# Elementwise work moved between engines, one-hot rows built by fours, a re-priced instruction planner, and 1200 unread products on TensorE

## The chip, the cores and the metric

The kernel runs on one core of one Trainium2 chip. The metric is the device time of one execution in microseconds (us), from launch to the last result, as the median of several executions. Engines are named as in the profile: PE is TensorE (PEld its weight loads), DVE is VectorE, ACT is ScalarE, POOL is GpSimd, SP is SyncE, whose queue issues most DMA transfers.

## What is computed

Two layers of a small transformer over 256 latent tokens and 256 context tokens, width 1024. In layer 0 both streams pass a token mixer and a PEER feed-forward layer; in layer 1 the context passes only as much of the mixer as the latents read.

```python
def peer_ffn(h, wq, keys, u_tab, v_tab):
    ...
    q = (t @ wq).reshape(n, PEER_HEADS, 2, PEER_HALF)
    s = jnp.einsum('thcd,cnd->thcn', q, keys).astype(F32)
    sv, si = lax.top_k(s, PEER_TOPK)
    cand = (sv[:, :, 0, :, None] + sv[:, :, 1, None, :]).reshape(n, PEER_HEADS, PEER_TOPK * PEER_TOPK)
    cv, ci = lax.top_k(cand, PEER_TOPK)
    ...
        act = jax.nn.gelu(jnp.einsum('pd,ped->pe', tb, u_tab[eb]), approximate=False)
        return jnp.einsum('pe,ped->pd', act * gb, v_tab[eb])

def reference(...):
    for l in range(DEPTH):
        ...
        m, mc = token_mixer(h, hc, ...)          # three branches and a gated merge
        x = x + gt1 * m
        x = x + gt2 * peer_ffn(modulate(x, norm2_g[l], sh2, sc2), ...)
        if need_ctx:
            xc = xc + gt1c * mc
            xc = xc + gt2c * peer_ffn(modulate(xc, norm2_g[l], sh2c, sc2c), ...)
    return x
```

The mixer's branches are a differential attention (A), a windowed attention with a sink (B) and a gated delta rule over chunks (C). PEER picks 128 of 16,384 experts for each token; an expert is one row of `u_tab` and one of `v_tab`, 4 KB each.

## The kernel before

**Work and stages.** A matrix product in full precision is three products of halves: `split` (627) copies an operand on ACT into a rounded half `hi`, and a `tensor_tensor` subtraction gives the rest `lo`, on DVE or, where the caller says so, on POOL; `mm3` (651) then multiplies hi by hi, hi by lo and lo by hi. Weights come in tiles of 128x1024 (512 KB) from the SP queue. The stages follow each other as: mixer of the context in layer 0; its PEER routing (label "01 route" in this text: the context route); mixer of the latents in layer 0 while the context's experts are gathered; the latents' route and dense PEER in layer 0 beside the rest of the gathers; the context part of layer 1; the latents' mixer, route and dense PEER of layer 1.

**Gathered PEER (context, `peer_gather` 1638).** For each of two token blocks, 128 indirect DMAs on POOL fetch rows of `u_tab` into tiles `rows`, each followed by one product with a running sum on DVE (`scalar_tensor_tensor` rows<-rows,ga); then 128 indirect DMAs fetch rows of `v_tab`, which PE multiplies with small masks into `ps`. These phases are called U0, V0, U1, V1.

**Dense PEER (latents, `peer_dense` 1531).** All experts are computed: for each pair of expert tiles `first` (1545) loads two tiles of `u_tab`, splits them and makes 48 products of 256 columns (dU); later two tiles of `v_tab` are loaded and split, and 24 products of 512 columns are summed into four PSUM banks (dV). `pre` pairs of dU are done ahead of the first dV. What an expert weighs for a token is a matrix that `weights` (1500) builds: for each token one row of two one-hot vectors on DVE (`tensor_scalar` against `iota`, 128 columns) and one 128x128 product on PE, copied out on ACT and written to memory. This is the build.

**The order of the work.** Nothing is issued directly. `Rec` (280) records every operation, and `order` (386) plans all five engines' queues at once with priced operations (`cost`), priorities, a limited number of buffers (tags b4, b2, b1 in SBUF, ps in PSUM) and lanes; each engine then runs its queue in order, held by semaphores. `BORROW` lends buffers of one tag to the gather. NEAR, FAR, SPARE limit how far an operation may run ahead of its lane. An instruction's line in the profile is thus always that of the emitting helper, 603; groups are told apart by names and shapes.

**What the change touches.** The subtraction of a split on POOL: mixer weights by `wpool` (WPOOL, 47 of them, from the layer-0 latents' misc stage to their route), dU tiles by `up` (UP1, 32 in layer 1), dV tiles by VP (112 in layer 1). `gdn_chains` (1020), seven chains of the delta rule, scales 128x256 tiles by per-head columns on POOL (144 of them). `aux`, set to POOL for layer 1, does the small sums of `route` and the products in `decode`. `qk_prep`, `out_proj` add on POOL.

## Time and profile before

| | us |
|---|---|
| median of 3 executions | 3939.72 (3938.74 to 3962.46) |
| the profiled execution | 3933.92 |
| its span, first to last instruction | 3932.1 |
| PE busy | 3530.0 (90%) |
| DVE busy | 2472.8 (63%) |
| ACT busy | 1610.0 (41%) |
| POOL busy | 1481.9 (38%) |
| mean granted PE clock | 0.933 |

The profiled execution is read as the time of the kernel: span plus 1.8 us around it. A busy engine is one that has an instruction in flight; a product that streams at half clock counts as busy for twice as long. Idle time of PE is shown with the engine whose result ended it. Where stretches are named by A:B, they are us from the span's start.

### The profile page before, as it was taken

What the parts mean: (1) busy time and instruction counts of PE and PEld (TensorE: products, weight loads), DVE (VectorE), ACT (ScalarE), POOL (GpSimd) and SP (SyncE); (2) the same over time, 40 slices, a digit from 0 to 9 for tenths busy, and PEclk for the clock granted to TensorE, in tenths of its full rate; (3) what the DMA queues carried; (4) which work ended last, traced back from release to release, by engine and by line L of the source; (5) the groups of instructions that cost most, each with busy time, mean ns of one, the idle gap of its engine ahead of it and who ended that gap; (6) DMA issues with size and microseconds to landing.
All of it is one profiled execution on the core that took longest, in us unless ns stands there. A gap on an engine that the chain in (4) does not pass through costs nothing. (4 is left out here: it accounts for less than half of the span.)

```text
span 3932.1 us, 64402 instructions
## 1 busy us (share of the span) xinstructions
PE 3530.0 (90%) x24312; PEld 2982.5 (76%) x24312; DVE 2472.8 (63%) x5599; ACT 1610.0 (41%) x3070; POOL 1481.9 (38%) x1125
## 2 busy tenths in 40 slices
PE   7999964986997798889999999998996899899999
PEld 6787954866794467767777888877896699678998
DVE  4444579889656886897444454646559942555554
ACT  4544422433442233343333346544543343344443
POOL 1110123778364345663333202222023043675443
PEclk9999986877898999999999998988998999999999
DMA  7356742566466799999889851302351455565653
GB/s 279 112 169 239 254 168 98 184 230 233 161 206 231 252 368 376 384 409 361 334 332 333 310 195 43 103 28 89 103 197 65 129 184 170 190 222 213 221 207 142
DMA packets 300966, 837.78 MB, mean 213 GB/s; under 512 B 26736, under 2 KB 96752, under 8 KB 300656
## 3 DMA queue, kind: packets, MB, share of 16 engines
q1 hardware_dynamic: 153168, 522.80, 37.2%
q0 software_dynamic: 73728, 268.47, 18.6%
q10 hardware_dynamic: 73760, 42.40, 3.6%
q8 instruction: 192, 3.15, 0.3%
q14 instruction: 118, 0.97, 0.1%
HBM read 792.67 MB, written 40.89 MB: 212 GB/s over the span
## 5 line engine op out<-in xcount | busy, mean ns | idle before, releaser
L603 PE MATMUL ps<-b,b 128*128 128x256 f32 (+4 forms) x18528 | 2742.4, 309 | 202.7 <-DVE b L603 134.8
L603 PEld LDWEIGHTS ps<-b,b 128*128 128x128 f32 (+2 forms) x18528 | 2449.7, 192 | 476.8 <-DVE b L603 163.3
L603 DVE TENSOR_TENSOR b<-b,b 128x1024 fp32r<-128x1024 f32 (+3 forms) x1065 | 1142.8, 1106 | 817.2 <-ACT b L603 550.9
L603 ACT CAST b<-b 128x1024 fp32r<-128x1024 f32 (+1 forms) x982 | 917.4, 976 | 702.6 <-PE ps L603 297.9
L603 POOL TENSOR_TENSOR b<-b,b 128x1024 fp32r<-128x1024 f32 (+2 forms) x241 | 586.8, 2445 | 922.7 <-DVE b L603 367.5
L603 ACT COPY b<-ps 128x256 f32<-128x256 f32 (+3 forms) x896 | 291.2, 350 | 676.4 <-PE ps L603 666.6
L603 POOL DMA_INDIRECT rows<-in_u_tab,eid x256 | 357.8, 1398 | 271.1 <-DVE rows L603 118.2
L603 POOL DMA_INDIRECT rows<-in_v_tab,eidT x256 | 284.0, 1109 | 426.5 <-PE ps L603 354.6
L603 PE MATMUL ps<-b 128*128 128x128 f32 (+1 forms) x2048 | 337.9, 320 | 19.2 <-ACT b L603 7.5
L603 PE MATMUL ps<-consts,b 128*128 128x128 f32 (+1 forms) x1290 | 261.1, 316 | 103.8 <-DVE b L603 76.9
L603 ACT ACTIVATE b<-ps 128x512 f32<-128x512 f32 (+1 forms) x264 | 136.7, 520 | 523.5 <-PE ps L603 507.0
L603 PEld LDWEIGHTS ps<-b 128*128 128x128 f32 (+1 forms) x2048 | 255.7, 207 | 119.6 <-DVE b L603 39.6
L603 DVE SCALAR_TENSOR_TENSOR rows<-rows,ga 128x1024 f32<-128x1024 f32 x256 | 322.9, 1288 | 4.4 <-DMA rows<-in_u_tab,eid 2.4
L603 PEld LDWEIGHTS ps<-consts,b 128*128 128x128 f32 x1290 | 184.4, 180 | 148.2 <-issue 68.8
L603 DVE TENSOR_SCALAR b<-consts,b 128x128 f32<-128x128 f32 x1024 | 235.4, 309 | 10.8 <-DMA gd<-b 7.7
L603 PE MATMUL ps<-rows,ga 128*32 128x512 f32 x1024 | 160.5, 626 | 19.0 <-DMA rows<-in_v_tab,eidT 17.8
L603 DVE COPY_PREDICATED b<-masks,ps 128x64 f32<-128x64 uint8 (+1 forms) x416 | 83.7, 251 | 148.5 <-PE ps L603 146.9
L603 ACT COPY b<-b 128x128 f32<-128x128 f32 x384 | 108.0, 303 | 60.5 <-DVE b L603 56.1
L603 DVE TENSOR_TENSOR b<-ps,b 128x128 f32<-128x128 f32 (+4 forms) x144 | 61.9, 454 | 93.8 <-PE ps L603 57.8
L603 PEld LDWEIGHTS ps<-rows,ga 128*32 128x32 f32 x1024 | 29.5, 111 | 94.6 <-DMA rows<-in_v_tab,eidT 47.8
L603 PE MATMUL ps<-b,cs 128*32 128x256 f32 x768 | 69.8, 430 | 12.2 <-DVE cs L603 11.5
L603 ACT ACTIVATE b<-b 128x512 f32<-128x512 f32 (+1 forms) x62 | 38.9, 629 | 96.0 <-DVE b L603 42.5
(176 smaller groups left out, 1450.6 us busy)
## 6 DMA issues: line engine op xcount, KB each, us to landing
b<-in_u_cols SPq DMA_DIRECT2D x256, 512.0 KB
b<-in_v_tab SPq DMA_DIRECT2D x256, 512.0 KB
b<-in_w_in SPq DMA_DIRECT2D x184, 512.0 KB
gd<-b ACTq DMA_DIRECT2D x64, 512.0 KB
b<-gd SPq DMA_DIRECT2D x64, 512.0 KB
b<-in_w_ada SPq DMA_DIRECT2D x48, 512.0 KB
b<-in_w_ada SPq DMA_DIRECT2D x96, 256.0 KB
b<-in_wq SPq DMA_DIRECT2D x48, 512.0 KB
```

The source lines that it names most:

```text
L603: r = getattr(getattr(nc, o.eng), o.meth)(*[_real(x) for x in o.args], **{k: _real(x) for k, x in o.kw.items()})
```

## The change

Splits are all on DVE (WPOOL, UP0, UP1 empty, VP 1), as are the additions of `qk_prep` and `out_proj` and the small sums of layer 1's route. The chains' scalings become two ACT instructions of 128 columns in place of one POOL instruction of 256. One-hots are built four tokens at a time: the first vector of four tokens in one DVE `tensor_tensor`, three of the four second vectors by DVE as before, the fourth by two ACT instructions (Abs, Relu). The planner prices operations anew, knows of a port between DVE and POOL, gives borrowed slots back earlier, lets marked operations run ahead of FAR, and has other limits; PRE is 32 in place of 48. One PSUM bank is taken from `ps` (8 to 7) for products of two constant tiles that nothing reads; `rests` counts them from the planner's own idle time of PE, and `emit` puts them ahead of the product that is to wait.

```diff
-WPOOL = (1, 3, 5, 7)
-UP0, UP1 = (), range(0, 64, 4)
+WPOOL = ()
+UP0, UP1 = (), ()
-OUTV = False
+OUTV = True
-VP = 8
+VP = 1
+
+ACTB = (1, 1)
+TAIL, FREE1 = 0, True
+FREE = {"b4": 4, "b2": 2, "b1": 1, "ps": 0}
-PRE = 48
+PRE = 32
+WARM0, WARM = 20.0, 0.75
-NEAR, FAR = 20.0, 150.0
+NEAR, FAR, URGENT = 20.0, 80.0, 0.0
...
+        o.port = eng in ("vector", "gpsimd") and not o.dma and sum(
+            isinstance(x, V) and x.n > 1 and x.tile.kind == "sb" for x in ins) > 1
...
+    def rests(self, order):
+
+        out, end = {}, 0.0
+        for when, i in order:
+            o = self.ops[i]
+            if o.eng == "tensor":
+                if when > WARM0:
+                    out[i] = int(max(0.0, when - end - 0.3) * WARM / 0.24)
+                end = when + o.dur
+        return out
+
     def emit(self):
...
+            for _ in range(rests.get(i, 0)):
+                nc.tensor.matmul(bank, w.real(), x.real(), start=True, stop=True)
...
-        self.bufs = {"ps": 8, "psg": 2, "b4": B4, "b2": B2, "b1": B1}
+        self.bufs = {"ps": 7, "psg": 2, "b4": B4, "b2": B2, "b1": B1}
...
-                nc.gpsimd.tensor_tensor(m1, M1[:, None, :].to_broadcast([P, H2, P]), bc(gc), op=OP.mult)
+                for h in range(H2):
+                    nc.scalar.activation(m1[:, h], M1, AF.Copy, scale=gc[:, h:h + 1])
...
+                nc.vector.tensor_tensor(A[:, :, 0], io4, sc[:, 1, k:k + 4, None].to_broadcast([P, 4, P]), op=OP.is_equal)
                 for t in range(4):
                     k = t0 + q + t
-                    nc.vector.tensor_scalar(A[:, t, 0], self.iota, sc[:, 1, k:k + 1], None, OP.is_equal)
-                    nc.vector.tensor_scalar(A[:, t, 1], self.iota, sc[:, 0, k:k + 1], sc[:, 2, k:k + 1],
-                                            OP.is_equal, OP.mult)
+                    if t >= ACTB[l]:
+                        nc.vector.tensor_scalar(A[:, t, 1], self.iota, sc[:, 0, k:k + 1], sc[:, 2, k:k + 1],
+                                                OP.is_equal, OP.mult)
+                    else:
+
+                        d = A[:, t, 1]
+                        nc.scalar.activation(d, self.iota, AF.Abs, scale=-1.0, bias=sc[:, 0, k:k + 1])
+                        nc.scalar.activation(d, d, AF.Relu, scale=sc[:, 3, k:k + 1], bias=sc[:, 2, k:k + 1])
...
-        self.aux = self.nc.gpsimd
+        pass
         self.lab("1 norm1")
+        self.nc.free = FREE1
```

Counted in the built program: POOL has 1130 instructions before and 721 after, DVE 4913 and 4666, ACT 3046 and 3592, PE 21074 and 23474 (1200 products into `warm` and as many weight loads). Of the 1200, 217 stand in two runs in the context route (155 and 62), 162 in layer 1's route (160 of them in one run), 159 in 18 places before V0's products, 160 in 29 places in layer 0's dense PEER, and the other 502 in places of at most 34.

**The build in layer 1, DVE's queue.** `b` tiles are the one-hots, `consts` the iota. Before:

```order
L603 TENSOR_TENSOR b_5773_30349<-io_8_159,pjf_30347 128x1024
L603 TENSOR_SCALAR b_5787_30357<-consts_71,b_5777_30336 128x128 x4
L603 TENSOR_SCALAR b_5789_30362<-consts_71,b_5777_30336 128x128 x4
L603 TENSOR_SCALAR b_5791_30367<-consts_71,b_5777_30336 128x128 x2
L603 TENSOR_REDUCE pii_29622<-b_5774_30355 128x2x16 x2
```

After, DVE and then ACT:

```order
L642 TENSOR_TENSOR pgw_31668<-pgw_31668,psm_31685 128x256
L642 TENSOR_TENSOR b_5791_31648<-consts_72,b_5781_31646 128x4x128
L642 TENSOR_TENSOR b_5793_31652<-consts_72,b_5781_31646 128x4x128
L642 TENSOR_SCALAR b_5791_31648<-consts_72,b_5781_31646 128x128 x3
L642 TENSOR_SCALAR b_5793_31652<-consts_72,b_5781_31646 128x128 x3
```

```order
L642 ACTIVATE b_5845_31976<-consts_72,b_5781_31646 128x128
L642 ACTIVATE b_5845_31976<-b_5845_31976,b_5781_31646 128x128
L642 COPY b_5829_31955<-ps_31970 128x64x4
L642 COPY b_5830_31960<-ps_31970 128x64x4
L642 ACTIVATE b_5847_31990<-consts_72,b_5781_31646 128x128
L642 ACTIVATE b_5847_31990<-b_5847_31990,b_5781_31646 128x128
```

Eight DVE instructions for four tokens became four, and ACT got two beside its two copies out of PSUM.

**The dV stretch of layer 1, DVE's queue.** A 128x1024 row is the subtraction of a tile's split, the 128x2x128 and 128x512 rows are the weights' product and split for a pair. Before (the other tiles' subtractions are in POOL's queue):

```order
L603 TENSOR_TENSOR b_6534_35213<-b_6534_35213,b_6536_35030 128x2x128
L603 TENSOR_TENSOR b_6538_35246<-b_6534_35213,b_6537_35235 128x512
L603 TENSOR_TENSOR b_6552_35276<-b_6552_35276,b_6535_35012 128x2x128
L603 TENSOR_TENSOR b_6552_35276<-b_6552_35276,b_6536_35030 128x2x128
L603 TENSOR_TENSOR b_6554_35296<-b_6552_35276,b_6553_35289 128x512
L603 TENSOR_TENSOR b_6567_35302<-b_6565_35207,b_6566_35293 128x1024
```

After:

```order
L642 TENSOR_TENSOR b_6604_36754<-b_6604_36754,b_6606_36356 128x2x128
L642 TENSOR_TENSOR b_6634_36777<-b_6632_36526,b_6633_36744 128x1024
L642 TENSOR_TENSOR b_6608_36791<-b_6604_36754,b_6607_36773 128x512
L642 TENSOR_TENSOR b_6622_36811<-b_6622_36811,b_6605_36316 128x2x128
L642 TENSOR_TENSOR b_6622_36811<-b_6622_36811,b_6606_36356 128x2x128
L642 TENSOR_TENSOR b_6624_36829<-b_6622_36811,b_6623_36824 128x512
L642 TENSOR_TENSOR b_6637_36851<-b_6635_36566,b_6636_36795 128x1024
```

All subtractions stand in one queue now, and POOL's has none.

**The context route, PE's queue.** PE has done the hi parts of a projection and needs the `lo` of a weight tile (b_1358), which DVE makes. Before:

```order
L603 MATMUL ps_6422<-b_1201_4431,b_1331_6412 128x128 x4
L603 MATMUL ps_6487<-b_1192_5780,b_1357_6477 128x256
L603 MATMUL ps_6487<-b_1193_5783,b_1357_6477 128x256
L603 MATMUL ps_6538<-b_1192_5780,b_1375_6529 128x256
L603 MATMUL ps_6538<-b_1193_5783,b_1375_6529 128x256
L603 MATMUL ps_6487<-b_1192_5780,b_1358_6607 128x256
```

After, the end of the run of 155 pairs of a weight load and a product into `warm`, which stands at this place:

```order
L634 LDWEIGHTS idb_158
L634 MATMUL warm<-e_10_164,idb_158 128x512
L642 MATMUL ps_6443<-b_1192_5900,b_1358_6722 128x256
L642 MATMUL ps_6443<-b_1192_5900,b_1357_6092 128x256
L642 MATMUL ps_6443<-b_1193_5916,b_1357_6092 128x256
```

In DVE's queue, 13 of U0's row products stand ahead of the route's last instruction before, and 4 after. By the 7000th of PE's 20,928 planned products, 228 of the 512 gathers have been issued before, and 264 after; by the 9000th, 389 and 396.

## Rows read from the trace of the kernel before

**Rows 1.** The page: busy times over the span.
```profile
PE 3530.0 (90%) x24312; PEld 2982.5 (76%) x24312; DVE 2472.8 (63%) x5599; ACT 1610.0 (41%) x3070; POOL 1481.9 (38%) x1125
```
**Rows 2.** Stretches: length, busy PE, PEld, DVE, ACT, POOL; PEclk, DMA share, GB/s.
```profile
505.00:690.00 185.00, 94.87 (x704) 90.33 (x705) 162.58 (x610) 51.74 (x86) 51.36 (x39) 0.73 0.36 122
690.00:1080.00 390.00, 332.12 (x2166) 280.26 (x2166) 314.18 (x612) 155.78 (x410) 268.21 (x221) 0.80 0.61 202
...
1495.00:1900.00 405.00, 366.21 (x2209) 311.82 (x2210) 335.68 (x497) 155.09 (x185) 217.11 (x150) 0.98 0.96 372
...
2330.00:2910.00 580.00, 544.02 (x4223) 481.63 (x4222) 328.23 (x714) 307.00 (x790) 119.39 (x152) 0.92 0.26 88
2910.00:3048.00 138.00, 92.93 (x731) 90.97 (x729) 110.38 (x476) 47.39 (x69) 42.58 (x57) 0.84 0.28 98
3048.00:3170.00 122.00, 110.82 (x523) 77.64 (x524) 121.80 (x518) 41.98 (x131) 5.32 (x2) 0.95 0.48 135
```
**Rows 3.** PE's waits in 505:690: us in total, times, longest.
```profile
PE ps L603 <- DVE b L603: 85.3, 8, 29.1
PE ps L603 <- ACT b L603: 5.9, 5, 1.6
```
**Rows 4.** PEld's waits in 1080:1335.
```profile
PEld ps L603 <- DMA rows<-in_v_tab,eidT: 42.9, 26, 4.4
```
**Rows 5.** Eight stretches at half clock, columns as in rows 2, two and the sum of all.
```profile
731.80:759.10 27.30, 27.30 (x142) 21.90 (x141) 18.99 (x51) 10.13 (x43) 17.84 (x20) 0.50 0.52 168
...
2390.70:2424.80 34.10, 34.10 (x188) 25.99 (x188) 8.43 (x40) 15.40 (x67) 4.28 (x8) 0.50 0.01 1
sum 225.20, PE 145.57 PEld 112.71 DVE 151.41 ACT 66.98 POOL 53.93; mean PE 18.20 PEld 14.09 DVE 18.93 ACT 8.37 POOL 6.74
```
**Rows 6.** Groups by shape in 1900:2180: count, busy us, mean ns, idle before.
```profile
L603 DVE TENSOR_TENSOR b<-b,b 128x1024 fp32r<-128x1024 f32 x81 | 96.5, 1223 | 68.9 <-ACT b L603 46.4 <-PE ps L603 14.5 <-issue 7.7
```
**Rows 7.** The same in 3540:3900.
```profile
L603 POOL TENSOR_TENSOR b<-b,b 128x1024 fp32r<-128x1024 f32 x61 | 172.8, 2845 | 192.0 <-ACT b L603 76.4 <-DVE b L603 56.1 <-PE ps L603 49.5
L603 DVE TENSOR_TENSOR b<-b,b 128x1024 fp32r<-128x1024 f32 x73 | 149.3, 2063 | 76.0 <-ACT b L603 62.7 <-PE ps L603 12.8
```
**Rows 8.** PE's groups by shape in 3340:3540.
```profile
L603 PE MATMUL ps<-b,b 128*128 128x512 f32 x680 | 173.3, 413 | 17.5 <-POOL b L603 10.3 <-DVE b L603 4.0 <-ACT b L603 2.9
L603 PE MATMUL ps<-b,b 128*128 128x256 f32 x67 | 8.4, 284 | 1.5 <-DVE b L603 1.5
```
**Rows 9.** PE's groups by shape in 3560:3880.
```profile
L603 PE MATMUL ps<-b,b 128*128 128x256 f32 x1370 | 165.1, 281 | 0.0
L603 PE MATMUL ps<-b,b 128*128 128x512 f32 x680 | 160.0, 394 | 0.0
```
**Rows 10.** Groups by shape in 3048:3170, the build of layer 1.
```profile
L603 DVE TENSOR_SCALAR b<-consts,b 128x128 f32<-128x128 f32 x512 | 117.6, 305 | 0.2 <-ACT b L603 0.2
L603 PE MATMUL ps<-b 128*128 128x128 f32 x512 | 109.0, 323 | 4.0 <-DVE b L603 0.9
...
L603 ACT COPY b<-ps 128x256 f32<-128x256 f32 x130 | 42.1, 376 | 81.0 <-PE ps L603 81.0
```
**Rows 11.** DVE's groups by shape, whole span.
```profile
L603 DVE TENSOR_TENSOR b<-b,b 128x512 f32<-128x512 f32 x18 | 12.3, 689 | 3.1 <-ACT b L603 2.7
```
**Rows 12.** ACT's groups by shape, whole span.
```profile
L603 ACT COPY b<-b 128x128 f32<-128x128 f32 x384 | 108.0, 303 | 60.5 <-DVE b L603 56.1 <-DVE gS L603 2.5 <-ACT b L603 1.1
...
L603 ACT ACTIVATE b<-ps 128x256 f32<-128x256 f32 x96 | 36.6, 384 | 59.3 <-PE ps L603 56.4 <-issue 0.8 <-DVE b L603 0.5
...
L603 ACT ACTIVATE b<-ps,modT,A 128x256 f32<-128x256 f32 x48 | 24.3, 563 | 22.5 <-PE ps L603 20.7 <-issue 1.7
```
**Rows 13.** POOL's groups by shape, whole span.
```profile
L603 POOL TENSOR_TENSOR b<-b,b 128x1024 fp32r<-128x1024 f32 x191 | 505.8, 2658 | 597.0 <-PE ps L603 245.8 <-ACT b L603 227.6 <-DVE b L603 66.7
...
L603 POOL TENSOR_TENSOR b<-consts,gd_g 128x256 f32<-128x256 f32 x56 | 39.0, 717 | 18.2 <-DVE gd_g L603 14.1 <-ACT b L603 4.1
```
**Rows 14.** DVE's groups by shape in 505:1080.
```profile
L603 DVE SCALAR_TENSOR_TENSOR rows<-rows,ga 128x1024 f32<-128x1024 f32 x128 | 170.2, 1359 | 0.0
```

More of the change, by code (lines that the diff above doesn't have):

```diff
@@ L265 @@
     __slots__ = ("i", "eng", "meth", "args", "kw", "dur", "dma", "preds", "succ", "tiles", "prio",
-                 "npred", "ready", "lab", "lane", "cw")
+                 "npred", "ready", "lab", "lane", "cw", "port", "free")
 NAMES = []
@@ L316, in cost @@
             return max(c * n, 140 if dt == BF else 64) / 2330.0, 0
-        big = max([n] + [x.n for x in ins if isinstance(x, V)])
-        ps = any(isinstance(x, V) and x.tile.kind == "ps" for x in list(ins) + [out])
+        vs = [x for x in ins if isinstance(x, V)]
+        big = max([n] + [x.n for x in vs])
+        ps = any(x.tile.kind == "ps" for x in vs + [out])
+        ptrs = sum(x.n == 1 for x in vs)
         if eng == "scalar":
-            ptr = any(isinstance(kw.get(x), V) for x in ("scale", "bias"))
-            return (0.05 if ps else 0.095) + (0.08 if ptr else 0.0) + big / 1200.0, 0
+            both = all(isinstance(kw.get(x), V) for x in ("scale", "bias"))
+            acc = 0.1 if kw.get("accum_out") is not None else 0.0
+            return (0.05 if ps else 0.095) + (0.19 if both else 0.09 if ptrs else 0.0) + acc + big / 1200.0, 0
@@ L322, in cost @@
         if eng == "vector":
-            two = sum(isinstance(x, V) and x.n > 1 for x in ins) < 2 and not ps and meth in (
-                "tensor_scalar", "tensor_copy", "tensor_single_scalar")
-            if meth == "tensor_tensor" and out.dt == BF and all(x.dt == BF for x in ins if isinstance(x, V)):
+            wide = [x for x in vs if x.n > 1]
+            two = len(wide) < 2 and not ps and not ptrs and meth in ("tensor_scalar", "tensor_copy", "tensor_single_scalar")
+            if meth == "tensor_tensor" and out.dt == BF and all(x.dt == BF for x in vs):
@@ L326, in cost @@
                 two = True
-            ptr = (0.11 if meth == "tensor_scalar" else 0.06) if any(isinstance(x, V) and x.n == 1 for x in ins) else 0.0
-            return (0.125 if ps else 0.065) + ptr + big / (1920.0 if two else 960.0), 0
+            base = 0.065 if not ps or len(wide) > 1 else 0.125
+            if meth in ("max_index", "match_replace") or any(x.dt in (I32, U32) for x in vs):
+                base += 0.06
+            c = base + 0.06 * bool(ptrs) + big / (1920.0 if two else 960.0)
@@ L441, in order @@
         started = np.zeros(N + 1, bool)
-        together, last_out, pe_at = {}, None, 0.0
+        together, last_out, pe_at, port = {}, None, 0.0, 0.0
         def push(o):
@@ L538, in order @@
                         pe_at = at
+                    if o.port:
+                        at = max(at, port)
+                        port = at + o.dur
                     busy[e] = fin = at + o.dur
@@ L590, in order @@
         return out
+    def rests(self, order):
[7 more added lines that the diff above has]
+        return out
     def emit(self):
         nc = self.nc
-        for when, i in self.order():
+        order = self.order()
+        rests = self.rests(order)
+        bank, w, x = self.warm
+        for when, i in order:
             o = self.ops[i]
+            for _ in range(rests.get(i, 0)):
+                nc.tensor.matmul(bank, w.real(), x.real(), start=True, stop=True)
             for t in o.tiles:
```

70 lines of the change are left out of this document (44 added, 26 removed).

## The prediction, made before the run

> **What bounds the kernel now.** I read the page first: PE is busy for 3530.0 of 3932.1 us [rows 1], so it is the engine to follow, and at most 402 us are open idleness. Then the stretches [rows 2], since the share is a mean over stages with different limits. In each the reader asks which engine is nearly full. In 505:690 (context route) PE is busy for 94.87 of 185 us and DVE for 162.58; PE's waits there are 85.3 us on DVE [rows 3]. In 690:1080 (latents' mixer, beside the gather) DVE has 314 of 390, POOL 268, and PE 332 at a granted clock of 0.80. In 1495:1900 the DMA share is 0.96. In 2910:3170 (route and build of layer 1) DVE has 110 of 138 and 121.80 of 122. The stretches left out (0:505, 1080:1186, 1900:2330, 3540 on) have PE at 94% or more.
>
> The third reading is of the clock. Eight stretches at 0.50, half of 2.4 GHz, last 225 us together and have 145.57 us of busy PE in them [rows 5]. They are of two kinds: in some PE waits, and in others, as 731.8:759.1, it is busy for 27.30 of 27.30 us and still runs at half.
>
> The fourth is of the same instruction beside POOL and without it. The subtraction of a split, 128x1024, takes DVE 1223 ns in 1900:2180, where POOL only issues gathers [rows 6], and 2063 ns in 3540:3900, where POOL makes the same kind of subtraction in 2845 ns [rows 7]. So the two do not run side by side: what POOL took over, DVE pays for in part by waiting.
>
> **The change part by part**, against the profiled execution, 3933.9 us (5.8 below the median of 3939.7, inside the spread of the three).
>
> *Splits back on DVE, dV stretch of layer 1.* In 3340:3540 PE made 680 products of 512 columns and 67 of 256 [rows 8]. At its own pace they take 160.0/680 = 0.235 and 165.1/1370 = 0.1205 us each [rows 9], 168 us in all; the window is 200. The 32 us went to waits, POOL first (10.3 us of the open ones), the rest hidden in products that are in flight but starved. After, a pair of tiles costs DVE two subtractions at 1.223, and three smaller instructions at no more than 0.689 each [rows 11]: 4.5 us against 24 x 0.235 = 5.6 on PE. DVE covers it with 1.1 us to spare. **-32** (bounds -32 and 0). In the rest of the dense stage PE is full [rows 9] and nothing is to be had.
>
> *Build by fours, two layers.* Before: 512 DVE instructions, 117.6 us of a stretch of 122 [rows 10]. After, for each of 64 groups: one of 512 columns at 0.689 and three at 117.6/512 = 0.230, so 88 us. ACT: two copies at 42.1/130 = 0.324, and two one-hot steps. A 128-column copy takes 0.303; two pointers add 563 - 384 = 179 ns [rows 12], so one adds about 90 (estimate): 0.393 and 0.482. That makes 1.52 us a group, 97 in all: ACT is late next. PE was busy for 109.0, part of it starved. So the gain lies between 9 (PE's 109 is its own need) and 21 a layer; I take 15, in the middle, twice. **-30** (bounds -42 and -18, with nothing in layer 0: -9).
>
> *Small sums of layer 1's route back on DVE.* 48 instructions: 8 of about a thousand columns at 1.223 at most, and 40 of under 33 columns, for which 0.305 [rows 10] is an upper bound: 22 us on the queue that ends this stage. POOL's round trips go. **+12** (0 to 22).
>
> *Context route.* Nine fewer of U0's row products stand ahead of the route's end on DVE, 1.359 us each [rows 14], in a stage where PE waits for DVE: **-12**.
>
> *Layer-0 mixer.* 47 splits come to DVE, 47 x 1.223 = 57 us between 505 and 1335; most lie beside PE-bound work: **+10** (0 to 57). Against it, the row products there take 1.359 and a free 128x1024 takes 1.223: 128 x 0.136 = 17 us of port waits gone, and POOL's queue, where chain steps stood behind gathers, holds none of them: **-15** (-17 to 0).
>
> *Chains' scalings on ACT.* 288 instructions at 0.303 + 0.090 = 0.393: 113 us on ACT, for 144 at 0.717 [rows 13], 103 us, off POOL. Step by step 0.786 replaces 0.717: 144 x 0.07 = 10 us at most on the chain. In 2330:2910, with four of the seven chains, ACT goes from 307 to about 372 of 580, far from full. **+5** (0 to 10). The Trainium skill (ScalarE: Activation LUTs, Rules for kernel authors) speaks against this: it puts multiplications on VectorE, and prices a ScalarE instruction at about 0.3 us and 0.83 ns an element. By it the 288 would cost 118 us in place of 113, and the choice would be 144 on VectorE at no more than 0.689, 99 us; the trace agrees on the price, and its rows have VectorE as the fuller engine.
>
> *POOL out of layer 1's chains.* PE idles for 36 us of 580 there; POOL's in-order queue is one cause among several. **-10** (-36 to 0).
>
> *1200 unread products.* The trace has none; the nearest row is 512 columns at 0.235 [rows 9], so 282 us of PE if all were paid, and 0 if every one stood in a true wait. By place: 217 x 0.235 = 51 us in the context route, where PE waits for 85.3 - 12 = 73; 162, 38 us, in layer 1's route, where it idles for 138 - 92.93 = 45; 159, 37 us, before V0's products, where it waits 42.9 [rows 4]; 160, 38 us, in layer 0's dense stage, where it idles for 405 - 366 = 39 in 1495:1900, just as much; the other 502, 118 us, against some 190 of the 402 that remain. I charge half of the tight one: **+20** (0 to 156: the tight one and the scattered ones in full).
>
> *What they buy.* If PE never fell to half clock, the 145.57 us busy in the eight stretches would shrink by 73. The products stand in the waits, and few stand in the stretches that are full and cold. I take half of the bound: **-35** (0 to -73).
>
> *One PSUM bank fewer.* PE waits for ACT for 5.9 us in 185 [rows 3]; the same again over the mixers (690:1080 and 2330:2910, 970 us) would be 31. **+5** (0 to 31).
>
> *Gathers earlier.* 36 more are out by the 7000th product and 7 by the 9000th, so 29 x 0.524 MB = 15 MB leave the stretch with DMA share 0.96: 41 us at 372 GB/s, and PE idles for 39 there. **-20** (-39 to 0).
>
> Sum: -32 - 30 + 12 - 12 + 10 - 15 + 5 - 10 + 20 - 35 + 5 - 20 = -102, so 3933.9 - 102 = **3832 us**.
>
> **The rivals.** *A, the products are late, not idle time:* they are counted from planned waits, and where PE runs behind its plan the wait is gone and each costs 0.235 us in front of work that is ready. The place is layer 0's dense stage and the scattered ones, 662 in all: 156 us in place of 20, 3832 + 136 = 3968, slower than before. It decides from (102 + 20)/0.235 = 520 paid products. For it: the tight sum in 1495:1900, and PE at 98% and more in 1900:2330. Against: the three large places have waits that are longer than their fill. *B, DVE takes POOL's place as the bound:* the splits and sums come at full price (57 and 22) where DVE already has 314 of 390, the port waits prove small, and the gather's gain is nothing: -62 - 12 + 57 + 22 + 5 + 20 - 35 + 5 = 0, 3934, no change. For it: DVE in rows 2. Against: 2063 and 1223. *C, the clock holds throughout:* 73 in place of 35, no product is paid, and layer 0's dense stage loses all its idle time: -38 - 20 - 19, 3755. The Trainium skill (TensorE: Matmul & The Clock Gate, Part 4) says that transposes do not count as activity for the clock; by that rule plain products put among them would lift it, and C would be the time. The trace fits it as far as 731.8:759.1 is full and at half clock; no row has such a product in it. *D, the products do not do what they are for:* the full, cold stretches stay at 0.50, and in the waits the clock is up where nothing is streamed: 3832 + 35 = 3867.
>
> **How the numbers follow.** The forecast gets 0.45, C 0.20, D 0.13, B 0.12, A 0.10. The predicted time is the forecast's. The range goes from 3740, a little under C, to 3930, just under B, and leaves out A and half of B. About 1% is what a measurement of this kernel can tell from no change; faster means under 3900. Forecast, C and D fall there nearly whole, B and A seldom: 0.77. Within 1%: most of B, A's middle and the tails of the forecast, 0.15. Slower: A's upper half and unforeseen stalls of the new order, 0.08.
>
> **What would show it.** Right: the dV stretch's 512-column products at 0.235 with no wait on POOL; DVE's 128x1024 subtraction near 1223 ns everywhere; ACT at 90% or more in the builds and the one-hot rows at about 88 us on DVE; the context route's wait filled by `warm` products and less than 73 us of it left; a mean clock above 0.95. Wrong: PE's queue in layer 0's dense stage with `warm` products while DMA and DVE have delivered; DVE over 95% in 505:1335; a build that is no shorter because PE's fp32 products need the 109 us. What would break it most is a wait in the new order that no row of the old one has, since the planner's limits and prices changed together.

## The result and the profile after

The changed kernel takes 3835.0 us (median of 4, 3832.9 to 3837.4) against 3939.2 before (3933.2 to 3962.5): a ratio of 0.9734, interval 0.9693 to 0.9774, 104 us faster. The profiled execution spans 3831.2 us at a mean granted clock of 0.974, against 3932.1 at 0.933. The total was forecast at 3832. It is right only because large errors in its terms cancelled; the runs below show which.

The busy times of the changed kernel over its span, against [rows 1]:

```profile
PE 3631.0 (95%) x25402; PEld 3021.2 (79%) x25512; DVE 2449.8 (64%) x5352; ACT 1768.7 (46%) x3616; POOL 820.0 (21%) x716
```

POOL's busy time fell by 662 us, and DVE's, which took the work over, did not rise. PE's 3631 includes 267.6 us of unread products (1090 of the 1200 have a record).

The stages follow from the last instruction of each, found in the trace by each engine's order; lengths in us. The first two columns are the result, the others are experiments that are told below. "Same order" is an experiment in which every instruction keeps the changed kernel's place. A build ends with the issue of its last gate write on ScalarE's queue, which can stand well behind the build's own work.

| stage | before | after | no products, same order | no products, 8 banks | products in own bank, 8 banks | chains on GpSimd | 47 splits on GpSimd, same order |
|---|---|---|---|---|---|---|---|
| context mixer | 519.4 | 529.1 | 551.3 | 529.0 | 515.5 | 515.8 | 525.9 |
| context route | 145.3 | 125.3 | 125.0 | 130.0 | 132.5 | 126.5 | 127.4 |
| latents' mixer, layer 0 | 522.2 | 477.6 | 493.0 | 480.1 | 478.0 | 507.8 | 522.3 |
| latents' route, layer 0 | 148.0 | 164.2 | 168.9 | 172.7 | 168.9 | 169.8 | 166.4 |
| build, layer 0 | 160.2 | 148.8 | 149.2 | 184.7 | 186.6 | 154.2 | 149.3 |
| dense, layer 0 | 834.5 | 845.6 | 857.1 | 825.2 | 829.7 | 848.5 | 846.5 |
| mixers, layer 1 | 580.2 | 564.5 | 576.2 | 542.9 | 547.0 | 545.6 | 565.3 |
| route, layer 1 | 144.5 | 158.4 | 158.4 | 157.9 | 158.2 | 157.2 | 158.4 |
| build, layer 1 | 115.6 | 105.1 | 106.5 | 107.2 | 105.1 | 104.2 | 105.0 |
| dense, layer 1 | 759.6 | 709.9 | 709.9 | 707.4 | 707.3 | 707.7 | 710.0 |

After minus before: +10, -20, -45, +16, -11, +11, -16, +14, -10, -50, together -101. Two stages carry it, the latents' mixer and layer 1's dense stage, both of which GpSimd's splits left. Their windows before (length; busy PE, PEld, DVE, ACT, POOL; clock, DMA share, GB/s), and the dense stage after:

```profile
664.70:1186.90 522.20, 463.04 (x3249) 404.78 (x3247) 392.65 (x709) 216.97 (x498) 353.66 (x269) 0.85 0.61 203
3169.90:3929.50 759.60, 729.65 (x4516) 648.43 (x4514) 354.32 (x311) 320.07 (x376) 372.49 (x140) 0.98 0.55 195
```

```profile
3118.60:3828.50 709.90, 703.14 (x4430) 634.94 (x4431) 379.57 (x448) 314.20 (x372) 0.00 (x0) 1.00 0.57 199
```

In the mixer much of the gain is clock, 0.85 before and 0.97 after: length times clock is 444 us before and, with 102 unread products more, 463 after.

The dense stage also has fewer products than before (4430 and 4516 PE instructions): 196 of dU's stand ahead of it and not 108. At the 0.1205 us of [rows 9] these 88 are some 11 of its 50 us (an estimate); they are not gained, for they stand in the route and the build now.

The two builds are not what the table seems to say. From the route's end to the build's last copy on ScalarE, layer 0's takes 131.0 us before and 146.3 after, layer 1's 114.5 and 99.8. In layer 0 before, the last gate write was issued 28 us behind that copy. So the build by fours is shorter in layer 1 alone.

Windows of the changed kernel on the other stages and the mixer, same columns, against [rows 2]:

```profile
529.10:654.40 125.30, 105.76 (x678) 78.26 (x682) 112.11 (x528) 30.28 (x52) 16.61 (x16) 0.93 0.33 115
654.40:1132.00 477.60, 450.63 (x3407) 382.95 (x3435) 395.64 (x779) 236.68 (x578) 238.53 (x203) 0.97 0.71 251
1296.20:1445.00 148.80, 114.69 (x718) 77.28 (x725) 109.14 (x291) 87.26 (x254) 50.83 (x45) 0.94 0.83 275
1445.00:2290.60 845.60, 832.61 (x5298) 686.69 (x5315) 537.94 (x728) 336.31 (x409) 321.05 (x244) 1.00 0.89 338
2290.60:2855.10 564.50, 548.10 (x4267) 479.51 (x4286) 322.63 (x704) 331.51 (x909) 64.61 (x73) 0.95 0.27 92
3013.50:3118.60 105.10, 78.61 (x544) 69.44 (x545) 89.40 (x257) 81.06 (x250) 0.00 (x0) 0.94 0.58 167
```

PE is now busy for most of every stage but the builds, in the routes with products that nobody reads. In the dV stretch, PE's and DVE's groups by shape (window 3280:3450) show, against [rows 7] and [rows 8], what was forecast: no wait on POOL, and DVE's split at its free price.

```profile
L642 PE MATMUL ps<-b,b 128*128 128x512 f32 x724 | 168.3, 394 | 0.0
L642 DVE TENSOR_TENSOR b<-b,b 128x1024 fp32r<-128x1024 f32 x61 | 72.4, 1219 | 15.7 <-ACT b L642 15.7
L642 DVE TENSOR_TENSOR b<-b,b 128x256 f32<-128x256 f32 x56 | 20.0, 418 | 0.0
```

168.3/724 = 0.232 us, against 0.235 forecast.

PE's wait in the context route (529:654), against 85.3 us in [rows 3], and U0's row products in the latents' mixer (654:1132), against 1359 ns in [rows 14]:

```profile
PE ps L642 <- DVE b L642: 19.3, 2, 12.4
```

```profile
L642 DVE SCALAR_TENSOR_TENSOR rows<-rows,ga 128x1024 f32<-128x1024 f32 x124 | 149.4, 1229 | 3.8 <-DMA rows<-in_u_tab,eid 3.8
```

The wait is filled, not ended: the products stand in it. The row products now take 1229 ns, near the 1223 of an undisturbed instruction of this size.

### The profile page after: what moved, and what is told of

Its sections match the earlier page's. It is cut to its first block, busy times and chain, and to the rows that moved or that the text cites. A ratio compares the mean times of both kernels' runs of the same rounds, so it can differ in the third digit from the quotient of the medians.

```text
span 3831.2 us, 66072 instructions
## 1 busy us (share of the span) xinstructions
PE 3631.0 (95%) x25402; PEld 3021.2 (79%) x25512; DVE 2449.8 (64%) x5352; ACT 1768.7 (46%) x3616; POOL 820.0 (21%) x716
## 4 chain that ended last, share of the span: by engine, by line
PE 46%; DVE 4%; ACT 3%; issue 1%; ACTq 0%; POOL 0%; POOLq 0%; DMA 0%; DVEq 0%
PE ps L642 46%; ACT b L642 3%; DVE b L642 2%; ACTq L642 0%; DVE psi L642 0%; PE warm L634 0%; DVE psv L642 0%; DVE pii L642 0%; DVE dst L642 0%; DVE pS L642 0%; DVE pci L642 0%; ACT L642 0%; DVE pcd L642 0%; POOL qrs L642 0%; DVE pSi L642 0%
## 5 line engine op out<-in xcount | busy, mean ns | idle before, releaser
L642 PE MATMUL ps<-b,b 128*128 128x256 f32 (+5 forms) x18528 | 2685.9, 305 | 73.4 <-DVE b L642 43.9
L642 PEld LDWEIGHTS ps<-b,b 128*128 128x128 f32 (+2 forms) x18528 | 2415.5, 189 | 338.8 <-DVE b L642 67.8
L642 DVE TENSOR_TENSOR b<-b,b 128x1024 fp32r<-128x1024 f32 (+3 forms) x1282 | 1212.8, 988 | 726.3 <-ACT b L642 545.4
L642 PE MATMUL ps<-b 128*128 128x128 f32 (+1 forms) x2048 | 290.5, 307 | 60.5 <-ACT b L642 52.1
L634 PE MATMUL warm<-e,idb 128*128 128x512 bf16 x1090 | 267.6, 382 | 5.9 <-issue 2.4
L642 PE MATMUL ps<-consts,b 128*128 128x128 f32 (+1 forms) x1290 | 232.0, 291 | 29.5 <-DVE b L642 21.7
L634 PEld LDWEIGHTS <-idb 128*128 128x128 bf16 x1200 | 111.9, 99 | 133.8 <-issue 26.5
L642 DVE TENSOR_TENSOR b<-consts,b 128x512 f32<-128x512 f32 x128 | 87.8, 688 | 45.8 <-DMA gd<-b 32.6
L642 DVE TENSOR_SCALAR b<-consts,b 128x128 f32<-128x128 f32 x384 | 110.7, 346 | 0.0
L642 POOL TENSOR_TENSOR b<-b,b 128x512 f32<-128x512 f32 x24 | 45.1, 1880 | 291.6 <-DVE b L642 270.6
```

What stands on the lines that cost most here:

```text
L634: nc.tensor.matmul(bank, w.real(), x.real(), start=True, stop=True)
L642: r = getattr(getattr(nc, o.eng), o.meth)(*[_real(x) for x in o.args], **{k: _real(x) for k, x in o.kw.items()})
```

## The experiments

Medians in us, each beside the kernel before in the same session. The four sessions ran on four chips, and the changed kernel itself was timed in a session of its own, with an interval of 0.9693 to 0.9774, 16 us to either side. So a total that lies within some 16 us of 3835 is not told apart from it; what is said of smaller differences rests on the stages of the traces. e1, e3, e6 and e12 keep the changed kernel's order; for the others the planner made a new one.

| run | median | before there | ratio, interval |
|---|---|---|---|
| e1 no products | 3904.1 | 3940.3 | 0.991 (0.989 to 0.994) |
| e2 no products, 8 banks | 3838.2 | 3940.3 | 0.973 (0.968 to 0.979) |
| e3 dV splits on GpSimd | 3882.4 | 3940.3 | 0.985 (0.980 to 0.991) |
| e4 before, splits on VectorE | 3916.8 | 3940.3 | 0.995 (0.991 to 0.998) |
| e5 products in own bank | 3833.2 | 3938.6 | 0.970 (0.966 to 0.975) |
| e6 products in waits only | 3843.2 | 3938.6 | 0.975 (0.971 to 0.979) |
| e7 gate writes on SyncE | 3817.6 | 3938.6 | 0.968 (0.964 to 0.972) |
| e8 chains on GpSimd | 3839.6 | 3938.6 | 0.974 (0.970 to 0.979) |
| e9 combined | 3798.6 | 3945.3 | 0.962 (0.959 to 0.965) |
| e10 old one-hots | 3839.2 | 3945.3 | 0.972 (0.969 to 0.976) |
| e11 mixer splits on GpSimd | 3925.3 | 3945.3 | 0.994 (0.991 to 0.996) |
| e12 the same, old places | 3880.2 | 3921.7 | 0.990 (0.988 to 0.992) |

### The products and their bank (e1, e2, e5, e6)

**e1**

```diff
-WARM0, WARM = 20.0, 0.75
+WARM0, WARM = 20.0, 0.0
```

> The changed kernel without its 1200 unread products; every other instruction stands in the same order, and the bank that they wrote to stays unused. The sum of the prediction (products cost 20 us, the clock they hold gives 35): 3835 + 15 = 3850 us, mean granted clock about 0.95, most of it lost between 505 and 1335 and in layer 1's route. First rival, the clock is worth its whole bound (73 us, since the time at half clock fell from 13% to 5% of the span): 3835 - 20 + 73 = 3888, clock near 0.935. Second rival, the products ahead of V0's row products and in layer 0's dense stage are paid (35 us and more) and buy nothing: 3800 to 3825 us.

3904 us: without the products the kernel is 69 us slower, near the first rival. Windows of e1, columns as above:

```profile
0.00:551.30 551.30, 511.33 (x4012) 419.00 (x4013) 255.76 (x549) 257.45 (x652) 47.37 (x56) 0.90 0.55 192
551.30:676.30 125.00, 57.85 (x466) 56.50 (x464) 112.14 (x529) 30.34 (x52) 16.69 (x16) 0.74 0.33 114
676.30:1169.30 493.00, 445.40 (x3306) 388.15 (x3305) 398.39 (x778) 237.19 (x578) 233.43 (x203) 0.91 0.69 243
1487.40:2344.50 857.10, 814.51 (x5157) 682.92 (x5158) 538.54 (x728) 335.97 (x409) 327.15 (x246) 0.97 0.88 333
2344.50:2920.70 576.20, 547.59 (x4182) 485.96 (x4181) 322.84 (x704) 331.40 (x909) 64.36 (x73) 0.91 0.26 90
```

The context mixer of the changed kernel, and PE's wait in the context route of e1:

```profile
0.00:529.10 529.10, 500.60 (x4096) 408.01 (x4111) 255.49 (x549) 257.52 (x652) 47.37 (x56) 0.96 0.58 200
```

```profile
PE ps L642 <- DVE b L642: 67.2, 3, 45.8
```

Compare with the windows of the changed kernel. In the context route 216 recorded products raise the clock from 0.74 to 0.93 and take 48 of the 67.2 us of waiting, and the stage stays at 125 us: VectorE ends it either way. The same holds in layer 1's route (195 products, 158.4 and 158.4). What the products give, 22, 15, 5, 12 and 12 us, they give in the stages in which PE is the bound, and where only 79, 102, 178, 141 and 84 of them stand: there the clock is 0.90 to 0.97 without them and 0.95 to 1.00 with them. Not all of this is clear of chance: e3, e6 and e12, whose instructions in these stages are the changed kernel's (but for the products that e6 leaves out, and the engine of e12's splits), have 519 to 526 us in the context mixer, 166 to 171 in the latents' route and 846 to 853 in the dense stage. Against those, the gain in the context mixer, in layer 0's mixer (483 in e3 and e6) and in layer 1's mixers (565 in all three) stands, the 5 us of the route do not, and the dense stage's 12 hardly. So the stages with the long waits that the products fill are not made shorter; the gain lies in the mixers, where PE is the bound. Whether it comes from the few products there or from entering those stages with the clock up, e1 does not separate.

**e2**

```diff
-        self.bufs = {"ps": 7, "psg": 2, ...
+        self.bufs = {"ps": 8, "psg": 2, ...
```

(and no `warm` bank, no products)

> As the kernel before it (no products), and the eighth PSUM bank is given back to the tiles; the planner then makes its order with eight banks. The sum of the prediction: 5 us below the run without products. Rival, the bank was worth the bound of 31 us over the mixers: 25 to 35 us below it. Other rival, no difference within 4 us.

3838 us, 66 below e1 in the same session, over twice the bound of 31. Two windows of e2, layer 1's mixers and layer 0's build:

```profile
2321.70:2864.60 542.90, 514.24 (x4177) 459.14 (x4176) 323.90 (x709) 329.04 (x908) 63.92 (x73) 0.97 0.28 95
1311.80:1496.50 184.70, 121.56 (x796) 93.12 (x796) 131.47 (x324) 91.25 (x256) 80.32 (x74) 0.80 0.91 315
```

In layer 1's mixers the clock is 0.97 without a product; with seven banks it was 0.91. Length times clock is 527 us here and 576.2 x 0.91 = 524 in e1, equal within the rounding of the clock: the 33 us lie in the clock. The build only looks 36 us longer: its own work takes 149.4 us (146.8 in e1), but its last gate write is issued 34 us behind the last copy (1461.2 and 1495.3), and the dense stage behind it is shorter by nearly as much (825.2, 857.1). What is gained lies in the three mixers, 68 us. The bank and the new order come together here, and no run takes them apart.

**e5**

```diff
+            if rests.get(i, 0):
+                for sl, q in line.items():
+                    k = sum(t.ap is not None for t in q)
+                    if k < len(q) and (k == 0 or last[q[k - 1]] < p):
+                        free.append((last[q[k - 1]] if k else -1, sl, q[k]))
...
+                    for _ in range(rests[i] * 512 // max(n, 128)):
+                        nc.tensor.matmul(y, w.real()[:, :m], x.real()[:, :n], start=True, stop=True)
```

(and eight banks for `ps`; `y` is the bank that the next tile of that slot will take)

> Eight banks for tiles, as in the run without products that gave 3838 us, and the unread products are there, but each group of them is written into the bank that its next tile is about to take, so no bank is set aside. Theory that products and bank are two separate terms of about 66 us (products worth 69 in the order with seven banks, the eighth bank worth 66): both are had at once, 3838 - 55 = 3783 us or a little above, mean clock 0.97. Rival, the products only mend what the seven-bank order makes worse: 3838 us within 10, with the clock at 0.97 all the same. Other rival, products wait for the release of the bank and come late: over 3850 us.

3833 us at a clock of 0.977: the first rival. 69 and 66 do not add: products without the eighth bank, the eighth bank without products, and both come to the same time, within the intervals. One window more, layer 1's mixers of e5:

```profile
2311.20:2858.20 547.00, 531.25 (x4325) 469.03 (x4324) 323.63 (x709) 329.66 (x908) 63.91 (x73) 0.98 0.28 94
```

547.0 against e2's 542.9: where the clock is up already (0.97, and 0.98 with them), 148 more PE instructions bring nothing and the stage is 4 us longer. The Trainium skill (Perfetto Trace Analysis, Matmul Optimizations) advises that all 8 PSUM banks be used. The runs agree without products, where the eighth bank is worth 66 us, and not with them, where 3833 and 3835 do not differ.

**e6**

```diff
-            for _ in range(rests.get(i, 0)):
+            no = o.lab in ("0 ada0", "1 ada0", "01 V0", "01 V1", "00 dnorm", "00 didx", "00 dU", "00 dV")
+            for _ in range(0 if no else rests.get(i, 0)):
```

> The changed kernel in its own order, without the products that stand ahead of V0, V1, the sums of the norms, the index transposes, layer 0's dense stage and the first modulation products (about 420 of 1200; in the trace the groups ahead of V0's products leave no wait behind them). Rival A (they are late, paid at 0.235 us each): 3835 - 35 (V0) - 20 (the others) = 3780 us. The prediction's tight sum, 20 us of cost: 3815 us. Clock theory: they hold the clock for what follows, and without them the time rises to 3850 us or more.

3843 us, not told apart from the 3835 with them, and far from the 3780 of rival A, which is refuted: had the 409 products been paid and bought nothing, they would have cost 95 us, at the 0.232 us of a product of 512 columns. Ahead of V0's products the groups left no wait behind them in the trace, but without them that stage is not shorter (169.1 us; 164.2 to 171.1 with them). Dense layer 0 takes 853.0 us (845.6 to 852.8 with them), at 0.97 and not 1.00:

```profile
1447.60:2300.60 853.00, 815.19 (x5157) 682.88 (x5158) 537.61 (x728) 336.04 (x409) 321.04 (x243) 0.97 0.88 334
```

Whether they cost nothing or cost as much as their clock brought, e6 does not separate.

### GpSimd's splits (e3, e4, e12, e11)

**e3**

```diff
+            if o.lab == "10 dV" and o.meth == "tensor_tensor" and o.args[0].n == 1024:
+                self.nv = getattr(self, "nv", -1) + 1
+                if self.nv % 8:
+                    o.eng = "gpsimd"
```

> The changed kernel in its own order, but seven of eight subtractions of layer 1's dV stretch are issued on GpSimd, as before the change. Port theory at the prediction's size: 3835 + 32 = 3867 us. Port theory at the size that the traces of the two kernels show (the dense stage of layer 1 became 50 us shorter): 3885 us, with VectorE's 128x1024 subtraction there again near 2000 ns. Rival, the new order gained it and not the engine: 3835 us within 8.

3882 us, 47 more. In the profiled executions, which are 43 us apart, the stage itself went from 709.9 to 735.6 us, 26 more; the other 17 are a sum of gains and losses of up to 10 us in stages whose instructions did not change. The stage in e3:

```profile
3136.10:3871.70 735.60, 711.44 (x4430) 636.78 (x4431) 381.88 (x336) 315.87 (x372) 307.26 (x112) 0.99 0.53 192
```

Groups by shape of e3, window 3300:3480:

```profile
L646 PE MATMUL ps<-b,b 128*128 128x512 f32 x693 | 167.4, 401 | 12.9 <-POOL b L646 12.9
L646 DVE TENSOR_TENSOR b<-b,b 128x256 f32<-128x256 f32 x56 | 54.9, 1042 | 12.0 <-DMA b<-gd 12.0
L646 DVE TENSOR_TENSOR b<-b,b 128x1024 fp32r<-128x1024 f32 x7 | 12.9, 1848 | 0.0
```

PE waits for POOL again, and VectorE's own instructions stretch: 1848 ns for a split that took 1219, and 1042 for a 256-column product that took 418 in the changed kernel.

**e4**

```diff
-UP0, UP1 = (), range(0, 64, 4)
+UP0, UP1 = (), ()
...
-VP = 8
+VP = 1
```

> The kernel before, with only the two numbers changed that put layer 1's dU and dV splits on VectorE. Port theory at the prediction's size: 3939 - 32 = 3907 us; at the size that the traces show: 3889 us. Rival, the gain of that stage came from the rest of the change (order, clock, slots): 3939 us within 10.

3916.8 us: 22 us of gain (9 to 34), between nothing and the forecast's 32. The dense stage took 741.9 of 759.6, 18 less. The planner made a new order for e4, with 14 of dU's products ahead of the stage in place of 108, so the 18 us are no pure price of the engine: 94 products more at 0.1205 are 11 us, which would make it 29 (an estimate), beside e3's 26 in one order. With 26 for the engine and 11 for products that moved ahead, some 13 of the 50 are left and were not taken apart.

**e12** (the subtraction of every other weight tile of layer 0, 47 in all)

```diff
-WPOOL = ()
+WPOOL = (1, 3, 5, 7)
...
+            if self.nw % 8 in self.wpool:
+                POOLED.add(self.nc.ops[-1].i)
...
+            r = getattr(nc.gpsimd if i in POOLED else getattr(nc, o.eng), o.meth)(...)
```

> The changed kernel in its own order, but the same 47 weight splits of layer 0's mixer and route are issued on GpSimd. In the run before, where the planner made a new order for them, the time was 3925 us. If the engine and its queue make that loss (a split of 2.6 us held ahead of gathers and beside VectorE's port): 3900 us or more, with the stage between the context route's end and the end of layer 0's route over 660 us in place of 642. If the new order makes most of it: by the prediction's terms 3840 us; up to 3855 is counted to this side. Between the two: both.

3880 us, 45 more. It is the cleanest result here, for the order is kept and one stage moves: the mixer goes from 477.6 to 522.3 us, 45 more (522.2 in the kernel before), and no stage behind it differs by more than 2.2. In that session the kernel before took 3921.7 us, 18 less than elsewhere; by the ratios the loss is 64. The stage's window in e12:

```profile
653.30:1175.60 522.30, 466.11 (x3402) 397.13 (x3431) 407.36 (x739) 236.66 (x577) 325.13 (x240) 0.93 0.66 229
```

DVE's and POOL's split in that window:

```profile
L643 DVE TENSOR_TENSOR b<-b,b 128x1024 fp32r<-128x1024 f32 x42 | 78.4, 1868 | 15.2 <-ACT b L643 6.7 <-PE ps L643 6.0 <-POOL b L643 2.3
L643 POOL TENSOR_TENSOR b<-b,b 128x1024 fp32r<-128x1024 f32 x37 | 93.4, 2527 | 15.8 <-DVE b L643 8.2 <-ACT b L643 6.6 <-issue 0.5
```

PE's wait there, us in total, times, longest:

```profile
PE ps L643 <- POOL b L643: 27.9, 14, 5.6
```

The changed kernel's split on DVE in its own window of the stage, 654.4:1132:

```profile
L642 DVE TENSOR_TENSOR b<-b,b 128x1024 fp32r<-128x1024 f32 x82 | 102.0, 1267 | 5.0 <-ACT b L642 3.3 <-issue 1.4 <-PE ps L642 0.2
```

DVE makes 40 splits fewer and saves 24 us of them, but its busy time rises from 395.64 to 407.36: what POOL takes over comes back as longer instructions. PE waits 27.9 us for POOL and loses clock, 0.97 to 0.93. The Trainium skill (GPSIMD Engine Reference, Specifications) states that GpSimd's SBUF interfaces are shared with VectorE, with contention where a VectorE instruction has two SBUF inputs, as the subtraction has. The trace agrees: VectorE's subtraction goes from 1267 to 1868 ns. What GpSimd's would take alone, no run here shows.

**e11**

```diff
-WPOOL = ()
+WPOOL = (1, 3, 5, 7)
```

> The changed kernel with every other weight split of layer 0's mixer and route on GpSimd again, chains staying on ScalarE. By the prediction's terms (10 us cost on VectorE, 15 us of port waits gained): 3835 + 5 = 3840 us. Rival, these splits ahead of the gathers in GpSimd's queue are a good part of the 45 us by which that stage became shorter: 3855 us or more, the stage over 495 us. Other rival, VectorE is the fuller engine there and gains by it: below 3828 us.

3925 us, 90 more, where e12 has 45. By the ratios, which take out the two sessions' chips, it is 79 and 64. So the new order that the planner makes for it (build of layer 0 186.0 us, dense stage 877.1) costs something on top of the engine, between 15 and 45 us; no run settles how much.

### The builds (e10, e7)

**e10**

```diff
-                nc.vector.tensor_tensor(A[:, :, 0], io4, sc[:, 1, k:k + 4, None]..., op=OP.is_equal)
...
+                    nc.vector.tensor_scalar(A[:, t, 0], self.iota, sc[:, 1, k:k + 1], None, OP.is_equal)
```

(and all four second vectors on VectorE too)

> The changed kernel with the one-hots of the builds made one by one on VectorE as before, 512 instructions a layer; all else as changed. By the prediction's term: 3835 + 30 = 3865 us. By the two traces (the build of layer 0 became 11 us shorter, that of layer 1 10 us): 3857 us. Rival, a build by fours only trades VectorE's time for ScalarE's: 3835 us within 8.

3839 us, 4 more, which is the rival and no difference. In layer 1 the build is 14 us longer (118.9), as forecast; in layer 0 it is 12 us shorter (136.6). DVE in the build of layer 0, changed kernel (1296:1445):

```profile
L642 DVE TENSOR_TENSOR b<-consts,b 128x512 f32<-128x512 f32 x64 | 43.9, 687 | 39.7 <-DMA gd<-b 29.4 <-PE ps L642 9.5 <-ACT b L642 0.8
L642 DVE SCALAR_TENSOR_TENSOR rows<-rows,ga 128x1024 f32<-128x1024 f32 x18 | 21.2, 1221 | 0.0
```

18 of U1's row products stand in it (3 in e10), and VectorE waits 29.4 us until a written gate tile has landed. In e10 U1's row products end at 1800 us and not at 1753, and the dense stage behind takes 844.3 us against 845.6: having U1 done 47 us earlier bought nothing.

**e7**

```diff
-                nc.scalar.dma_start(G[t0 // P][h]...
+                nc.sync.dma_start(G[t0 // P][h]...
```

> The changed kernel with the writes of the gate matrix in the two builds issued by SyncE and not by ScalarE. Theory from the trace of the changed kernel: ScalarE ends the build by fours, 85 us of work and 15 us of holding its DMA issues in 110; without them a build is 10 to 15 us shorter, 3835 - 25 = 3810 us. Rival, TensorE's own 109 us is the floor of a build: 3835 within 8. Other rival, SyncE's queue stands behind the wait for the copies, so that the loads of the next stage come late: over 3845 us.

3818 us, 17 less by the medians and 22 by the ratios, at the edge of what the totals tell. The build of layer 1 takes 90.2 us in place of 105.1 (to its last copy, 89.2 and 99.8; the changed kernel's last write issue alone took 5.0), that of layer 0 145.2 and 148.8. Groups of the changed kernel in layer 1's build (3008:3119):

```profile
L642 DVE TENSOR_SCALAR b<-consts,b 128x128 f32<-128x128 f32 x192 | 54.7, 344 | 0.0
L642 ACT ACTIVATE b<-b,b 128x128 f32<-128x128 f32 x64 | 31.3, 495 | 16.0 <-issue 15.1
L642 ACT ACTIVATE b<-consts,b 128x128 f32<-128x128 f32 x64 | 25.0, 400 | 0.0
```

ACT's longest wait there:

```profile
ACT b L642 <- issue: 15.1, 14, 1.3
```

A piece of ACT's timeline (start, us, engine, what; in brackets the idle time before it):

```profile
3052.88 1.25 ACTq L642 DMA_DIRECT2D gd<-b  x2
3054.18 0.49 ACT L642 ACTIVATE b<-b,b 128x128 f32<-128x128 f32 x1 [1.05 <-issue]
```

This pair of DMA issues holds ScalarE's queue for 1.25 us; 14 such waits make 15.1 us in the build. With them on SyncE (e7, window 3019.3:3109.5) VectorE is busy throughout and ends the stage:

```profile
3019.30:3109.50 90.20, 78.09 (x527) 66.37 (x528) 90.15 (x259) 84.56 (x253) 0.00 (x0) 0.98 0.65 181
```

### The chains, and what can be had (e8, e9)

**e8**

```diff
-                for h in range(H2):
-                    nc.scalar.activation(m1[:, h], M1, AF.Copy, scale=gc[:, h:h + 1])
+                nc.gpsimd.tensor_tensor(m1, M1[:, None, :].to_broadcast([P, H2, P]), bc(gc), op=OP.mult)
```

(and likewise `m2`, `vb`, `kd`, `kg`)

> The changed kernel with the scalings of the chains on GpSimd as before the change, all else as changed. By the prediction's terms (10 us of chain saved by GpSimd, 5 lost on ScalarE's side, and 10 gained as GpSimd leaves layer 1's chains): 3835 - 5 to 3835 + 10. Rival, the move to ScalarE is what made the layer-0 mixer shorter (the stage to the attention's end went from 415 to 346 us): 3860 us or more. The planner makes a new order for it, which alone may move the time by some us.

3840 us, inside the forecast's -5 to +10, and again a sum of two large parts: layer 0's mixer is 30 us longer than after (507.8), layer 1's mixers 19 us shorter (545.6). A likely reason, not shown, for the planner's order is new too: in layer 0 GpSimd's queue holds the gathers (busy for 274.70 of 507.8 us), in layer 1 it is nearly empty (111.69 of 545.6), and one of its instructions does two of ScalarE's.

**e9**: e7, with layer 1's chains and the 48 sums of its route on GpSimd

```diff
-        pass
+        self.aux, self.cpool = self.nc.gpsimd, True
...
+                if on_pool:
+                    nc.gpsimd.tensor_tensor(m1, M1[:, None, :].to_broadcast([P, H2, P]), bc(gc), op=OP.mult)
```

> The changed kernel with three things: the gate matrix's writes on SyncE (which alone gave 3818 us), the 48 small sums of layer 1's route on GpSimd as before the change (the prediction charged 12 us for their move, and the stage is 13 us longer in the trace of the changed kernel), and the scalings of layer 1's chains on GpSimd as before, those of layer 0 staying on ScalarE (the run with all chains on GpSimd had layer 1's mixers in 546 us in place of 565, and layer 0's stage in 508 in place of 478). If the three add up: 3818 - 13 - 19 = 3786 us. Rival, the 19 us of the mixers come from another order and another course of the clock, not from the engine: 3805 us, with the stage at 560 or more. Other rival, the sums on GpSimd gain nothing: 3799 us.

3798.6 us, the fastest of all: 36 below the changed kernel (45 by the ratios), 19 below e7 (23). Layer 1's mixers take 556.0 us against e7's 573.0, 17 less, but only 8 less than the 564.5 of the changed kernel, whose chains are those of e7 in another order. The route takes 154.8 against e7's 156.8: the route's own VectorE instructions keep the engine busy for 93 us (320 of them) in place of 103 in the changed kernel (368), but VectorE waits for POOL instead (e9, window 2846.6:3001.4):

```profile
DVE pii L642 <- POOL b L642: 4.7, 3, 1.6
DVE pS L642 <- POOL b L642: 3.5, 3, 1.2
```

## Why the prediction was right, and where only its sum was

- **Splits back on VectorE, dV (-32): mechanism right, size near.** e3 shows 26 us in the stage, e4 22 in the time. The stage gained 50 in all, some 11 of it because products moved ahead of it.
- **Splits back on VectorE, layer-0 mixer (+10 - 15 = -5): wrong by 40.** The step "most lie beside PE-bound work: +10" took the 47 splits as a cost on VectorE, and the port waits as those of the row products alone, 17 us. e12 shows -45: the splits that stayed on VectorE were stretched too (1868 and 1267 ns), and PE waited 27.9 us for POOL's 2.5 us splits and lost clock for it.
- **Builds (-30): wrong in layer 0.** Layer 1 gave its 15 (114.5 to 99.8 us to the last copy; 14 in e10). VectorE's part came to 54.7 + 43.9 = 98.6 us and not 88, because 0.230 was the mean of two kinds of one-hot and the dearer kind is left: before, VectorE starts the next one 196 ns after a plain comparison and 256 after one with a product. ScalarE's 97 was right (40.7 + 31.3 + 25.0), but its DMA issues, 15 us, were not counted. In layer 0 the build became 15 us longer to its last copy (131.0 to 146.3; 135.6 with the old one-hots in e10), with waits for landed gate writes and U1's row products in it; the bound of 9 us "with nothing in layer 0" was the nearer one.
- **Unread products and the clock (+20 - 35 = -15): both ends mis-sized.** In the same order they give 69 net (e1), so the clock gives 69 or more, near its bound of 73 or above it. How many are paid is not separated; leaving out 409 of them changes nothing that can be told from chance (e6).
- **One PSUM bank fewer (+5): wrong, the largest miss.** Where no product stands in, the seven-bank order takes 66 more than the eight-bank order (e1, e2). I took PE's waits on ScalarE as the price; over the span they are 110.9 us with seven banks and 130.4 with eight, so that is not it. In layer 1's mixers the price is the clock. Since the products make up for just this, the two terms together are about -3 (3835 against e2's 3838), where I had -10: their net was near, by luck, for a reason that the prediction did not have.
- **Gathers earlier (-20): did not come.** Layer 0's dense stage is 11 us longer, and e10 shows that U1 47 us earlier is worth nothing. The 39 us of idle PE time that I gave it went to other things: PE is busy for 832.6 of 845.6 us, 36 of it unread products, and the stage is no shorter.
- **Context route (-12): -20 in the trace,** and the same 125 us without the products (e1); the order of the row products was not tested alone.
- **Layer 1's sums (+12):** 10 us of VectorE's time, near the forecast, but 2 of the stage (e9 against e7); the stage's 14 us are only partly theirs, since dU's splits now stand in it as well.
- **Chains (+5 - 10 = -5):** 5 in e8, which is not clear of chance, but as -30 in layer 0 and +19 in layer 1, the reverse of where I had placed the gain; the new order of e8 is in both. (The 118 us given there for 288 instructions comes out as 117.)

Of its signs, dV's products (0.232), the free subtraction (1242 ns over the span), the filled wait (19.3 us left) and the mean clock (0.974) came. ScalarE at 90% or more in the builds did not: it is busy for 81.06 of 105.1 us and for 87.26 of 148.8, as the queue was held by DMA issues or waited.

Of the rivals, A fell with e6. B was refuted by the total and by VectorE's busy time, 2449.8 us after and 2472.8 before. C's clock nearly came about (0.974) without its time, 3755: layer 0's dense stage lost none of its length. D holds in part: a full stretch still falls, as the last section shows.

What stays open: why the planner's order with eight banks keeps the clock at 0.97 in layer 1's mixers without a product, whether the bank or the order does it, how the gain of e1 divides between clock and paid products, and the 17 us of e3 outside its stage.

## What to carry to other kernels

Before work is put on GpSimd beside VectorE, compare the same VectorE instruction with and without it: here 47 subtractions of 2.5 us on GpSimd cost 45 us, because the neighbour's instructions stretched and TensorE waited for the slow ones. Filling TensorE's waits paid here in stages that TensorE itself ends and not in a stage that VectorE ends, and it is worth testing against simply giving the bank back: here the two came to the same. To price one part of a change, keep the order and swap the engine at the end; where the order is made anew, read the stages, not the total, and look at what ends a stage before its length is believed.

## What the runs showed of the hardware that was not expected

- The clock can fall in a stretch in which PE hardly waits. Windows 300:400 of e1 and of the changed kernel, and 100:200 of the changed kernel:

```profile
300.00:400.00 100.00, 94.04 (x556) 59.70 (x556) 30.39 (x94) 35.57 (x103) 4.92 (x6) 0.60 0.53 190
```

```profile
300.00:400.00 100.00, 94.25 (x770) 66.97 (x772) 41.31 (x107) 44.63 (x115) 6.16 (x7) 0.93 0.71 252
100.00:200.00 100.00, 98.60 (x750) 78.42 (x749) 47.68 (x155) 65.50 (x250) 3.09 (x6) 0.85 0.32 101
```

  PE is busy for 94 us in the first two, with 556 and 770 instructions, at 0.60 and 0.93. In the 100 us ahead it was busy for 88.67 us at 0.89 in e1 and for 95.52 at 1.00 in the changed kernel. So a busy PE alone does not tell its clock. (A clock of 0.50 is 1.2 GHz, 1.00 is 2.4; 0.60 is a mean of both.) No run shows what made it fall.
- Two DMA issues on ScalarE's queue hold it for 1.25 us, as long as three of its 128-column instructions of 0.40 us.
- VectorE's 256-column product of two SBUF tiles takes 418 ns, and 1042 in the stretch of e3 in which GpSimd subtracts: a factor of 2.5, where the 1024-column subtraction has 1.5.
